# A decoder trunk on one core: attention's last combination moved forward within u's projection, and v's gelu taken over four token tiles at once

## The chip, the cores and the metric

One core of a Trainium2 chip runs the whole program. The metric is the device time of one execution in microseconds, here the median of several runs; a profiled execution of the same program gives the trace from which all rows come. Engine names are those of the profile: PE is TensorE (matmuls), PEld its weight loads, ACT is ScalarE, DVE is VectorE, POOL is GpSimd, SP is the engine that issues the DMAs.

## The reference: what is computed

The program is a trunk of two residual layers on 1024 tokens of width 1024, in float32. The change lies in the mixer of the first layer. It projects the normalised input to five parts of 512 columns, u, v, q, k and vb. From u and v it makes a gated product, from q, k and vb a mixture of attention branches, and one output projection takes both, side by side:

```python
def chunked_gmlp(u, v, ln_g, ln_b, w_s, b_s):
    ...
    vn = layer_norm(v, ln_g, ln_b).reshape(Bn, nc, A_CHUNK, A_GROUPS, A_GROUP_DIM)
    ...
    mixed = jnp.einsum('gts,bnsgc->bntgc', ws, vn) + b_s.astype(jnp.float32).T[:, :, None]
    return u.astype(jnp.float32) * mixed.reshape(Bn, S, A_WIDTH)

def even_mixer(h, w_in, a_ln_g, a_ln_b, a_ws, a_bs, q_g, k_g, w_out):
    ...
    a_out = chunked_gmlp(jax.nn.gelu(u, approximate=False), jax.nn.gelu(v, approximate=False),
                         a_ln_g, a_ln_b, a_ws, a_bs)
    ...
    for window, dilation in B_BRANCHES:
        o_r, l_r = dilated_branch(qh, kh, vh, window, dilation)
    ...
    wts = jax.nn.softmax(jnp.stack(lses), axis=0)
    ...
    return jnp.concatenate([a_out, b_out], axis=-1).astype(h.dtype) @ w_out
```

Heads are worked off in four pairs of two. Two kinds of score blocks remain after merging branches: near ones (128 neighbouring tokens and those before) and dilated ones (every fourth token). The combination weighs the near output and the dilated output of a pair by the exponentials of their log-denominators.

## The kernel before

Tokens lie in eight tiles of 128 (n = 0 to 7). Each matmul operand in float32 is split into a high and a low part in a format that TensorE multiplies in one pass, and three of the four products are summed (PASSES, line 40). So one token tile times one 1024x512 weight is 24 matmuls of 128x512 (mm_tok, lines 182 to 191), and every weight or activation that TensorE reads costs ScalarE a cast (the high part, line 100 or 105) and VectorE a subtraction (the low part, line 101 or 106).

The last stage of the first mixer, which the change touches, runs from 272 to about 410 us:

- gmlp (574 to 610) projects v, tile by tile, into PSUM (pv). consume evacuates each tile with a gelu on ScalarE (line 591), and VectorE makes the layer norm of it: statistics (593, 595), a power on POOL (141), then three passes (597, 598, 600) into mx, of which there are two, one per half (four token tiles). When a half is full, eight small matmuls with the causal weights (pm, line 605) mix the tokens of each chunk, one per channel group, and VectorE adds the bias back into mx (606). pm shares two PSUM banks with attention's scores.
- The dilated score blocks of the last head pair run at the same time (dilated, 737; unit, 650): scores on TensorE (sc3d, 641), mask and row maximum on VectorE (646), exponentials on ScalarE (sm3d, 647), transposes on TensorE (pP3d, 661), a copy (pT3d, 664 or 666), the products with the values (po3d, 669), and after four blocks a copy to ot3d (748). ot3d goes to DRAM and comes back in token order as on (750, 788).
- u_proj (612 to 621) projects u into pu, evacuates with a gelu (ut, 616) and multiplies it into mx (617). At a chosen tile it calls last, which combines the last head pair: minima and differences (cM, cE, 759 and 762), an exponential on ScalarE (763), weights (770 to 773), the two scalings on POOL and VectorE (776), the sum (778), and a DMA to bcat (779).
- out_first (432 to 454) is the first half of the output projection. For each tile a DMA reads attention's half from bcat (cat, 1122), TensorE transposes mx and cat (pc, 442), the result is split into hq, and 24 matmuls (po, 190) follow. bcat has two halves of four token tiles each, and a cat tile holds columns of all four head pairs, so it needs the last pair's combination.

ScalarE has gelu and exponential in different function tables, and an ACT_TABLE_LOAD stands in its row wherever one follows the other. Copies and casts stand there without one.

The order of the work is not that of the code: a scheduler interleaves the independent chains on each engine, and the code's order only ranks them. An instruction marked keep_in_program_order is held back to its place in the code; the first step of the combination (cM) is marked so. Each engine then works off its own list strictly in order. The DMA issues of SP are one such list too.

Of the kernel before, what the change touches and what calls it, by code (L numbers as in the profile page):

```python
# [9 lines left out]
F32 = mybir.dt.float32  # L10
# [3 lines left out]
AF = mybir.ActivationFunctionType  # L14
ALU = mybir.AluOpType
# [4 lines left out]
P = 128  # L20
# [6 lines left out]
GROUPS = 8  # L27
# [19 lines left out]
def flat(t):  # L47
    return t.rearrange("p a b -> p (a b)")
# [7 lines left out]
def trunk(ctx: ExitStack, tc: tile.TileContext, a, out):  # L56
    nc = tc.nc
    V, A, G, T, Q = nc.vector, nc.scalar, nc.gpsimd, nc.tensor, nc.sync
# [5 lines left out]
    small = ctx.enter_context(tc.tile_pool(name="small", bufs=4, reuse_waits="tile"))  # L64
# [72 lines left out]
    def inv_rms(ssq, cols, n, name, r=None):  # L137
        if r is None:
            r = small.tile([P, cols], F32, tag="rs%d" % cols, name=name)
        G.tensor_scalar(r, ssq, 1.0 / n, EPS, op0=ALU.mult, op1=ALU.add)  # L140
        G.tensor_tensor(r, r, mhalf[:, :cols], op=ALU.pow)
        return r
# [431 lines left out]
    def gmlp(ps, gm):  # L574

        wv = load_half(a["w_vu"][0], "wv", g0)
        lnG = gm.tile([P, 512], F32, name="lnG")
        Q.dma_start(lnG, a["ln_g"].partition_broadcast(P))
        lnB = gm.tile([P, 512], F32, name="lnB")
        Q.dma_start(lnB, a["ln_b"].partition_broadcast(P))  # L580
        bs = gm.tile([P, GROUPS], F32, name="bs")
        Q.dma_start(bs, a["a_bs"])
        ws = gm.tile([P, GROUPS, P], F32, name="ws")
        Q.dma_start(ws, a["a_ws"])

        G.affine_select(out=ws, in_=ws, compare_op=ALU.is_ge, fill=0.0, base=0,
                        pattern=[[0, GROUPS], [1, P]], channel_multiplier=-1)

        def consume(n, pj):
            gv = gm.tile([P, 512], F32, tag="gv", bufs=2, name=f"gv{n}")  # L590
            A.activation(gv, pj, AF.Gelu, scale=r0[:, n : n + 1])
            st = small.tile([P, 6], F32, tag="bn", name=f"bn{n}")
            V.bn_stats(st, gv)
            mv = small.tile([P, 2], F32, tag="mv", name=f"mv{n}")
            V.bn_aggr(mv, st)
            r = inv_rms(mv[:, 1:2], 1, 1, f"lr{n}")
            V.tensor_scalar(gv, gv, mv[:, 0:1], r, op0=ALU.subtract, op1=ALU.mult)
            V.tensor_mul(gv, gv, lnG)
            half, j = n // 4, n % 4
            V.tensor_add(mx[half][:, j, :], gv, lnB)  # L600
            if j == 3:
                for g in range(GROUPS):
                    gc = mx[half][:, :, g * 64 : g * 64 + 64]
                    pm = ps.tile([P, 4, 64], F32, tag="sc", name=f"pm{half}{g}")
                    T.matmul(pm, ws[:, g, :], gc, start=True, stop=True)
                    V.tensor_scalar(gc, pm, bs[:, g : g + 1], None, op0=ALU.add)

        mx = [gm.tile([P, 4, 512], F32, name=f"mx{h}") for h in range(2)]
        proj512(ps, wv, "pv", consume)
        return [mx[n // 4][:, n % 4, :] for n in range(NT)]  # L610

    def u_proj(ps, gm, mixed, last):

        def consume(n, pj):
            t = gm.tile([P, 512], F32, tag="gv", bufs=2, name=f"ut{n}")
            A.activation(t, pj, AF.Gelu, scale=r0[:, n : n + 1])
            V.tensor_mul(mixed[n], mixed[n], t)
            if n == 4:
                last()

        proj512(ps, load_half(a["w_vu"][1], "wu", g0), "pu", consume)
# [489 lines left out]
    ps = banks(pss, mm=3, pt=2)  # L1111
# [148 lines left out]
```

## Time and profile before

| | us |
|---|---|
| median of 3 runs | 2196.88 |
| the runs | 2193.66 to 2197.9 |
| the profiled execution, its own time | 2195.83 |
| its span, first to last instruction | 2194.0 |
| TensorE busy | 2147.0 |
| VectorE busy | 1533.2 |
| ScalarE busy | 1042.7 |
| GpSimd busy | 489.0 |

The mean granted TensorE clock is 0.994. The rows below are read so: in the list of waits, who waited for whom, the total, how often, the longest; in the list in time, start, length, engine, line, operation, output and inputs, shapes, count, and in brackets the idle time before it with what ended it; in the groups, busy time, mean in ns, and the idle time ahead of them. f32 transposes and small products count two rows per instruction.

### The profile page before, as it was taken

The numbers are of one execution on the slowest core, as the hardware profiler recorded it, in microseconds if no ns is written. First come the engines' busy times: TensorE is split into PE (matmuls) and PEld (weight loads), VectorE is DVE, ScalarE is ACT, GpSimd is POOL, SyncE is SP. The second block draws the span as 40 slices with busy tenths as digits, with TensorE's granted clock in tenths as the row PEclk, the third lists the DMA queues.
The fourth block names the chain that finished last, engine by engine and source line by source line (L and its number), as shares of the span: only waits on it lengthen the run. The fifth ranks groups of instructions, "written<-read, shape, count | busy, mean of one in ns | idle before, by whom it ended". The sixth has DMA issues, their size and how long they took to land.

```text
span 2194.0 us, 29873 instructions
## 1 busy us (share of the span) xinstructions
PE 2147.0 (98%) x10508; PEld 1816.2 (83%) x10508; DVE 1533.2 (70%) x2459; ACT 1042.7 (48%) x2006; POOL 489.0 (22%) x519
## 2 busy tenths in 40 slices
PE   8999999899999999999999999999999999999999
PEld 8999987687888888878889788878788888888887
DVE  5566653567888788855577777667787878885554
ACT  6555664245444444444454455534544444454443
POOL 4444410003334342200010011110232424320000
PEclk9999999899999999999999999999999999999999
DMA  4122212565544444585563123377544454457555
GB/s 148 47 72 81 78 35 59 179 247 189 163 158 158 154 154 159 187 291 179 204 236 113 68 97 104 104 258 265 194 145 153 158 165 157 168 176 268 204 195 203
DMA packets 157254, 349.59 MB, mean 159 GB/s; under 512 B 17408, under 2 KB 54272, under 8 KB 156720
## 3 DMA queue, kind: packets, MB, share of 16 engines
q1 hardware_dynamic: 157104, 347.68, 46.9%
q8 instruction: 83, 1.36, 0.3%
q14 instruction: 67, 0.55, 0.1%
HBM read 239.02 MB, written 108.59 MB: 158 GB/s over the span
## 4 chain that ended last, share of the span: by engine, by line
PE 88%; DVE 4%; DMA 3%; ACT 3%; issue 1%; POOL 1%; SPq 0%; ACTq 0%; DVEq 0%
PE puB L290 11%; PE pgB L290 11%; PE po L190 7%; PE pj L190 6%; PE pgC L290 5%; PE puC L290 5%; PE pv L190 5%; PE pdB L397 5%; PE pdC L397 5%; PE pdO L397 4%; PE puA L290 3%; PE pgA L290 2%; PE pdP L397 2%; PE pdQ L397 2%; PE pBq L972 2%; PE pu L190 2%
## 5 line engine op out<-in xcount | busy, mean ns | idle before, releaser
L101 DVE TENSOR_TENSOR da<-ar,da 128x512 fp32r<-128x512 f32 x154 | 106.3, 690 | 156.2 <-ACT da L100 156.0
L100 ACT CAST da<-ar 128x512 fp32r<-128x512 f32 x154 | 95.9, 623 | 209.4 <-PE pdC L397 90.7
L190 PE MATMUL po<-wo,hq 128*128 128x512 f32 x768 | 186.4, 397 | 0.6 <-DVE hq L101 0.3
L190 PEld LDWEIGHTS po<-wo,hq 128*128 128x128 f32 x768 | 142.5, 189 | 30.2 <-DVE hq L101 1.4
L190 PE MATMUL pj<-wq,hq 128*128 128x384 f32 x768 | 157.8, 352 | 2.3 <-ACT vN L701 1.3
L190 PE MATMUL pv<-wv,hq 128*128 128x512 f32 (+2 forms) x768 | 141.1, 340 | 2.4 <-DVE b L1004 1.6
L190 PEld LDWEIGHTS pj<-wq,hq 128*128 128x128 f32 x768 | 135.3, 195 | 4.0 <-ACT vN L701 2.1
L397 PE MATMUL pdB<-dw,da 128*128 128x512 f32 x528 | 136.2, 391 | 0.9 <-ACT dw L100 0.9
L397 PE MATMUL pdC<-dw,da 128*128 128x512 f32 x528 | 135.8, 390 | 0.0
L190 PEld LDWEIGHTS pv<-wv,hq 128*128 128x128 f32 x768 | 118.7, 189 | 17.6 <-DVE b L1004 2.1
L397 PEld LDWEIGHTS pdB<-dw,da 128*128 128x128 f32 x528 | 98.7, 188 | 22.2 <-ACT dw L100 1.3
L397 PEld LDWEIGHTS pdC<-dw,da 128*128 128x128 f32 x528 | 99.0, 188 | 20.5
L256 POOL TENSOR_TENSOR S1g<-rg 128x512 f32<-128x512 f32 x20 | 29.3, 1464 | 384.2 <-DMA wsd<-D 325.0
L101 DVE TENSOR_TENSOR dw<-wr,dw 128x512 fp32r<-128x512 f32 x154 | 105.8, 687 | 10.7 <-ACT dw L100 10.4
L140 POOL TENSOR_SCALAR rn<-ssq 128x1 f32<-128x1 f32 x24 | 9.5, 397 | 461.3 <-ACT h L148 245.3
L397 PE MATMUL pdO<-dw,da 128*128 128x512 f32 x396 | 102.2, 389 | 0.2 <-DVE dw L101 0.2
L100 ACT CAST dw<-wr 128x512 fp32r<-128x512 f32 x154 | 95.0, 617 | 15.3 <-DMA wr<-in_w_dn 7.0
L397 PEld LDWEIGHTS pdO<-dw,da 128*128 128x128 f32 x396 | 74.3, 188 | 16.0 <-DVE dw L101 0.6
L319 DVE SCALAR_TENSOR_TENSOR t<-g,cw,t 128x1022 f32<-128x1022 f32 x44 | 75.6, 1719 | 0.1
L318 DVE SCALAR_TENSOR_TENSOR t<-g,cw,t 128x1023 f32<-128x1023 f32 x44 | 58.3, 1325 | 16.4 <-ACT t L317 16.4
L303 DVE TENSOR_TENSOR g<-g,s1g 128x512 f32<-128x512 f32 x22 | 16.2, 737 | 73.9 <-ACT s1g L302 73.9
L320 ACT ACTIVATE t<-t 128x1024 f32<-128x1024 f32 x44 | 46.7, 1061 | 29.8 <-DVE t L319 29.6
(1070 smaller groups left out, 5405.9 us busy)
## 6 DMA issues: line engine op xcount, KB each, us to landing
ar<-actd SPq DMA_DIRECT2D x70, 512.0 KB, 3.5
rd<-in_w_down SPq DMA_DIRECT2D x44, 512.0 KB, 3.6
wsd<-D SPq DMA_DIRECT2D x88, 256.0 KB, 2.6
rg<-in_w_gate SPq DMA_DIRECT2D x42, 512.0 KB, 3.6
ru<-in_w_up SPq DMA_DIRECT2D x42, 512.0 KB, 4.6
wr<-wsd SPq DMA_DIRECT2D x40, 512.0 KB, 4.5
actd<-t SPq DMA_DIRECT2D x66, 256.0 KB, 2.1
wr<-in_w_dn SPq DMA_DIRECT2D x30, 512.0 KB, 5.0
```

The lines of the kernel that those rows point to most:

```text
L100: (hi or A.copy)(dst[0], src)
L101: (lo or V.tensor_sub)(dst[1], src, f32(dst[0]))
L140: G.tensor_scalar(r, ssq, 1.0 / n, EPS, op0=ALU.mult, op1=ALU.add)
L190: T.matmul(o, L[i], R[jj][:, sl], start=(k == 0 and (ii, jj) == PASSES[0]), stop=(k == nk - 1 and (ii, jj) == PASSES[-1]))
L256: G.tensor_tensor(sums[name], x, y, op=op)
L290: T.matmul(o, L[ii][:, j * P : j * P + P], right[p][:, jj, j, :], skip_group_check=more, start=(not more and j == 0 and (ii, jj) == PASSES ...
L303: V.tensor_add(C22, C22, s1)
L318: V.scalar_tensor_tensor(t[:, 1:], g[:, : S - 1], w(1), t[:, 1:], op0=ALU.mult, op1=ALU.add)
L319: V.scalar_tensor_tensor(t[:, 2:], g[:, : S - 2], w(0), t[:, 2:], op0=ALU.mult, op1=ALU.add)
L320: A.activation(t, t, AF.Silu)
L397: T.matmul(o, L[ii][:, t * P : t * P + P], R[jj], skip_group_check=more, start=start and not more and (ii, jj) == PASSES[0], stop=stop and ...
L972: T.matmul(o, L[ii][:, j * P : j * P + P], right[p][:, jj, j, :], skip_group_check=more, start=(not more and j == 0 and (ii, jj) == PASSES ...
```

## The change

Three things change. The raw projection of v is copied (with its scale) into mx, and one gelu of 128x2048 follows when a half is full; the layer norm of its four tiles comes after it. The second half's gelu is marked to be held back to its place in the code, which is behind the attention of the last pair. u's gelus get a tag of their own with five buffers (they shared two with v's), and last is called behind tile 1 in place of tile 4.

```diff
         def consume(n, pj):
-            gv = gm.tile([P, 512], F32, tag="gv", bufs=2, name=f"gv{n}")
-            A.activation(gv, pj, AF.Gelu, scale=r0[:, n : n + 1])
-            st = small.tile([P, 6], F32, tag="bn", name=f"bn{n}")
-            V.bn_stats(st, gv)
-            mv = small.tile([P, 2], F32, tag="mv", name=f"mv{n}")
-            V.bn_aggr(mv, st)
-            r = inv_rms(mv[:, 1:2], 1, 1, f"lr{n}")
-            V.tensor_scalar(gv, gv, mv[:, 0:1], r, op0=ALU.subtract, op1=ALU.mult)
-            V.tensor_mul(gv, gv, lnG)
             half, j = n // 4, n % 4
-            V.tensor_add(mx[half][:, j, :], gv, lnB)
-            if j == 3:
-                for g in range(GROUPS):
...
+            A.activation(mx[half][:, j, :], pj, AF.Copy, scale=r0[:, n : n + 1])
+            if j < 3:
+                return
+            ge = A.activation(flat(mx[half]), flat(mx[half]), AF.Gelu)
+            if half:
+                tc.keep_in_program_order(ge)
+            for j in range(4):
+                gv = mx[half][:, j, :]
+                st = small.tile([P, 6], F32, tag="bn", name=f"bn{half}{j}")
+                V.bn_stats(st, gv)
+                mv = small.tile([P, 2], F32, tag="mv", name=f"mv{half}{j}")
+                V.bn_aggr(mv, st)
+                r = inv_rms(mv[:, 1:2], 1, 1, f"lr{half}{j}")
+                V.tensor_scalar(gv, gv, mv[:, 0:1], r, op0=ALU.subtract, op1=ALU.mult)
+                V.tensor_mul(gv, gv, lnG)
+                V.tensor_add(gv, gv, lnB)
+            for g in range(GROUPS):
...
-            t = gm.tile([P, 512], F32, tag="gv", bufs=2, name=f"ut{n}")
+            t = gm.tile([P, 512], F32, tag="ut", bufs=5, name=f"ut{n}")
             A.activation(t, pj, AF.Gelu, scale=r0[:, n : n + 1])
             V.tensor_mul(mixed[n], mixed[n], t)
-            if n == 4:
+            if n == 1:
                 last()
```

What the scheduler makes of it is seen in the engines' lists. First ScalarE around v's last tile and u's first. Before (gv7 is the gelu of v's last tile, sm3d1xx the exponentials of the second dilated half):

```order
L591 ACT_TABLE_LOAD
L591 ACTIVATE gv7_4314<-pv7_4289,r0_84 128x512
L105 ACTIVATE wu3_1_4379<-wu3r_4374,g0_83 128x512
L647 ACT_TABLE_LOAD
L647 ACTIVATE sm3d101_3883,ot3d1_3870<-sm3d101_3883,ot3d1_3870 128x128
L647 ACTIVATE sm3d110_3895,ot3d1_3870<-sm3d110_3895,ot3d1_3870 128x256
L748 COPY ot3d0_3781<-po3d0_3782 128x4x128
L647 ACTIVATE sm3d111_3903,ot3d1_3870<-sm3d111_3903,ot3d1_3870 128x256
```

The changed kernel at the same place (lines are five higher there):

```order
L591 ACTIVATE mx1_4005<-pv7_4253,r0_84 128x512
L105 ACTIVATE wu3_1_4373<-wu3r_4368,g0_83 128x512
L594 ACT_TABLE_LOAD
L594 ACTIVATE mx1_4005<-mx1_4005 128x2048
L652 ACT_TABLE_LOAD
L652 ACTIVATE sm3d100_3876,ot3d1_3870<-sm3d100_3876,ot3d1_3870 128x128
L669 COPY pT3d03_3861<-pP3d03_3844 128x512
L652 ACTIVATE sm3d101_3883,ot3d1_3870<-sm3d101_3883,ot3d1_3870 128x128
L652 ACTIVATE sm3d110_3895,ot3d1_3870<-sm3d110_3895,ot3d1_3870 128x256
L621 ACT_TABLE_LOAD
L621 ACTIVATE ut0_4401<-pu0_4376,r0_84 128x512
L753 COPY ot3d0_3781<-po3d0_3782 128x4x128
```

One gelu of four tiles stands where the eighth small one stood; all eight exponentials of the second dilated half come behind it, and u's first gelus stand between them, with a table load at each turn. From v's first tile to u's last, ScalarE's list holds 21 table loads before and 11 now.

Second, VectorE where the last combination begins. Before (pm1x are the mixed groups of the second half, ut4 the gelu of u's fifth tile):

```order
L606 TENSOR_SCALAR mx1_4005<-pm16_4344,bs_3999 128x4x64
L606 TENSOR_SCALAR mx1_4005<-pm17_4347,bs_3999 128x4x64
L617 TENSOR_TENSOR mx1_4005<-mx1_4005,ut4_4519 128x512
L759 TENSOR_TENSOR cM30_4522<-ot3n0_3177,on30_3959 128x8
L617 TENSOR_TENSOR mx1_4005<-mx1_4005,ut5_4579 128x512
```

In the changed kernel:

```order
L611 TENSOR_SCALAR mx0_4004<-pm07_4172,bs_3999 128x4x64
L622 TENSOR_TENSOR mx0_4004<-mx0_4004,ut0_4401 128x512
L622 TENSOR_TENSOR mx0_4004<-mx0_4004,ut1_4429 128x512
L764 TENSOR_TENSOR cM30_4432<-ot3n0_3177,on30_3959 128x8
L622 TENSOR_TENSOR mx0_4004<-mx0_4004,ut2_4489 128x512
L622 TENSOR_TENSOR mx0_4004<-mx0_4004,ut3_4517 128x512
```

The combination's first step moved ahead of u's third multiplication, and ahead of every bias pass of the second half.

Third, VectorE at the hand-over to the output projection (wo are its weights, hq00 and hq10 the split transposes of its first tile). Before:

```order
L101 TENSOR_TENSOR wo02_1_4695<-wo02r_4690,wo02_1_4695 128x512
L101 TENSOR_TENSOR wo03_0_4700<-wo03r_4698,wo03_0_4700 128x512
L617 TENSOR_TENSOR mx1_4005<-mx1_4005,ut7_4635 128x512
L101 TENSOR_TENSOR wo03_1_4703<-wo03r_4698,wo03_1_4703 128x512
L101 TENSOR_TENSOR hq00_85<-pc00_4660,hq00_85 128x4x128
```

In the changed kernel:

```order
L101 TENSOR_TENSOR wo03_0_4694<-wo03r_4692,wo03_0_4694 128x512
L611 TENSOR_SCALAR mx1_4005<-pm17_4341,bs_3999 128x4x64
L622 TENSOR_TENSOR mx1_4005<-mx1_4005,ut4_4545 128x512
L622 TENSOR_TENSOR mx1_4005<-mx1_4005,ut5_4573 128x512
L622 TENSOR_TENSOR mx1_4005<-mx1_4005,ut6_4601 128x512
L622 TENSOR_TENSOR mx1_4005<-mx1_4005,ut7_4629 128x512
L101 TENSOR_TENSOR wo03_1_4697<-wo03r_4692,wo03_1_4697 128x512
L101 TENSOR_TENSOR hq00_85<-pc00_4654,hq00_85 128x4x128
```

The last bias pass and all four multiplications of the second half now stand between the weights' splits and the first split of hq; on TensorE the last pm stands behind u's last matmul, directly ahead of the first pc.

More of the change, by code (lines that the diff above doesn't have):

```diff
@@ L589, in consume @@
         def consume(n, pj):
-            gv = gm.tile([P, 512], F32, tag="gv", bufs=2, name=f"gv{n}")
-            A.activation(gv, pj, AF.Gelu, scale=r0[:, n : n + 1])
-            st = small.tile([P, 6], F32, tag="bn", name=f"bn{n}")
-            V.bn_stats(st, gv)
-            mv = small.tile([P, 2], F32, tag="mv", name=f"mv{n}")
-            V.bn_aggr(mv, st)
-            r = inv_rms(mv[:, 1:2], 1, 1, f"lr{n}")
-            V.tensor_scalar(gv, gv, mv[:, 0:1], r, op0=ALU.subtract, op1=ALU.mult)
-            V.tensor_mul(gv, gv, lnG)
-            half, j = n // 4, n % 4
-            V.tensor_add(mx[half][:, j, :], gv, lnB)
-            if j == 3:
-                for g in range(GROUPS):
[L603 to L606, printed above, removed]
+            half, j = n // 4, n % 4
+            A.activation(mx[half][:, j, :], pj, AF.Copy, scale=r0[:, n : n + 1])
[15 more added lines that the diff above has]
+            for g in range(GROUPS):
+                gc = mx[half][:, :, g * 64 : g * 64 + 64]
+                pm = ps.tile([P, 4, 64], F32, tag="sc", name=f"pm{half}{g}")
+                T.matmul(pm, ws[:, g, :], gc, start=True, stop=True)
+                V.tensor_scalar(gc, pm, bs[:, g : g + 1], None, op0=ALU.add)
         mx = [gm.tile([P, 4, 512], F32, name=f"mx{h}") for h in range(2)]
```

## The prediction

> **What bounds the kernel now.** The page's head comes first.
>
> ```profile
> span 2194.0 us, 29873 instructions
> PE 2147.0 (98%) x10508; PEld 1816.2 (83%) x10508; DVE 1533.2 (70%) x2459; ACT 1042.7 (48%) x2006; POOL 489.0 (22%) x519
> ```
>
> TensorE is the bound, so an edit on other engines gains only what TensorE idles, or runs slowly, because of them. The change touches the stretch from v's projection (272 us) to the first output tiles (about 410 us). The second view is the waits on TensorE there: who waited for whom, total, times, longest.
>
> ```profile
> PE pc L442 <- DMA cat<-bcat: 9.3, 1, 9.3
> PE pP3d L661 <- ACT sm3d L647: 3.3, 3, 2.0
> PE pu L190 <- ACT ut L616: 0.9, 1, 0.9
> PE pv L190 <- ACT gv L591: 0.5, 2, 0.3
> PE pv L190 <- ACT vN L701: 0.3, 1, 0.3
> ```
>
> So 14.3 us are lost there, 9.3 of them in one wait: the transposes of the first output tile need attention's half (cat), which a DMA reads from bcat. Third, TensorE in order of time (start, length, work; idle before it and its releaser in brackets).
>
> ```profile
> 310.32 0.39 PE L661 MATMUL pP3d<-ident,sm3d 128*128 128x128 f32 x2
> ...
> 338.66 0.47 PE L661 MATMUL pP3d<-ident,sm3d 128*128 128x128 f32 x1 [2.04 <-ACT sm3d L647]
> ...
> 339.64 4.56 PE L190 MATMUL pu<-wu,hq 128*128 128x512 f32 x15
> ...
> 368.94 4.59 PE L190 MATMUL pu<-wu,hq 128*128 128x512 f32 x19 [0.88 <-ACT ut L616]
> ...
> 393.56 0.60 PE L442 MATMUL pc<-ident,mx 128*128 128x128 f32 x4
> 403.41 1.12 PE L442 MATMUL pc<-ident,cat 128*128 128x128 f32 x4 [9.25 <-DMA cat<-bcat]
> ...
> 408.63 5.14 PE L190 MATMUL po<-wo,hq 128*128 128x512 f32 x19
> ```
>
> The reader is to see that equal rows last unequally: 19 matmuls take 4.59 us at 368.94 (0.24 us each) and 5.14 at 408.63; 15 take 4.56 at 339.64, where 0.24 each makes 3.62. The fourth view, by stretches, says why: its PEclk column is the granted clock (third from the end, ahead of DMA share and GB/s).
>
> ```profile
> 336.00:338.00 2.00, 0.62 (x4) 0.38 (x3) 1.77 (x5) 1.98 (x3) 0.19 (x1) 1.00 0.86 277
> 338.00:341.00 3.00, 2.34 (x7) 2.00 (x8) 2.34 (x6) 2.97 (x11) 0.55 (x1) 0.52 0.78 266
> ...
> 396.30:403.40 7.10, 0.00 (x0) 0.00 (x0) 2.93 (x5) 0.00 (x0) 0.00 (x0) 0.50 0.96 292
> 403.40:409.60 6.20, 5.94 (x19) 4.65 (x20) 1.98 (x3) 2.24 (x4) 0.00 (x0) 0.50 0.96 375
> 409.60:413.60 4.00, 4.00 (x18) 3.22 (x17) 0.69 (x1) 0.00 (x1) 0.00 (x0) 0.98 0.26 67
> ```
>
> After the 2.04 us gap the clock is half (0.52) for 3 us; after the long gap it stays half for 6.2 us of work. A gap thus costs its length and some slow matmuls behind it.
>
> **The combination, moved.** It is the chain that ends in the 9.25 us. Its stations now, and the DMA groups (KB each, us to landing):
>
> ```profile
> 359.26 0.59 ACT L748 COPY ot3d<-po3d 128x512 f32<-128x512 f32 x1 [5.23 <-PE po3d L669]
> ```
> ```profile
> 362.39 1.52 SPq L788 DMA_DIRECT2D on<-od  x2
> 393.23 0.36 SPq L779 DMA_DIRECT2D bcat<-ot3n  x1
> ...
> 397.82 0.47 SPq L1122 DMA_DIRECT2D cat<-bcat  x1
> ```
> ```profile
> 386.53 0.16 DVE L759 TENSOR_TENSOR cM<-ot3n,on 128x8 f32<-128x8 f32 x1
> ```
> ```profile
> cat<-bcat SPq DMA_DIRECT2D x4, 256.0 KB, 5.6
> ...
> on<-od SPq DMA_DIRECT2D x2, 264.0 KB, 3.3
> ```
>
> The data (on) is back at 362.39 + 1.52 + 3.3 = 367.2, but VectorE's first step (cM) starts at 386.53, behind u's fifth multiplication. From there to cat's landing at 403.4 it is 16.9 us. The order of the changed kernel puts cM behind u's second multiplication. That stands 75 u-matmuls and 8 small matmuls (pm) before the end of u: 75 x 0.24 + 8 x 0.25 = 20 us, less one bias pass and two multiplications (about 1.8 us), so 18 us ahead of it. If u ends at 387.4 (below), cM starts at 369.4. What it waits for: the last dilated outputs come 102 u-matmuls and 11 pm before that end, 27.2 us, so at 360.2; their copy ends near 361.0, and the round trip that takes 7.3 us now (359.85 to 367.2) ends at 368.3. That is 1 us of margin. Even if the rest again takes 16.9 us, cat lands at 386.3, before its transposes at 388.0. The 9.25 us go. Queued behind cM on VectorE are u's third and fourth multiplications and the bias passes that free pm's banks; a late "on" would hold these. On SP the loads of the second output half (wo10r to wo13r) now come behind cat; they are needed only near 452 us, and TensorE is busy without a break until then, so I cost that at nothing.
>
> **v's gelu in blocks of four.** Its rows on ScalarE, and four of the engine's list in time:
>
> ```profile
> L647 ACT ACT_TABLE_LOAD x9 | 11.5, 1283 | 12.1 <-DVE ot3d L646 6.5 <-DVE ot3n L646 5.5
> L591 ACT ACT_TABLE_LOAD x8 | 10.3, 1283 | 0.1
> ...
> L591 ACT ACTIVATE gv<-pv,r 128x512 f32<-128x512 f32 x8 | 5.5, 688 | 5.5 <-PE pv L190 5.5
> ...
> L616 ACT ACT_TABLE_LOAD x3 | 3.8, 1283 | 0.3 <-PE pu L190 0.3
> ```
> ```profile
> L320 ACT ACTIVATE t<-t 128x1024 f32<-128x1024 f32 x44 | 46.7, 1061 | 29.8 <-DVE t L319 29.6
> ```
> ```profile
> 299.93 1.28 ACT L647 ACT_TABLE_LOAD   x1 [5.49 <-DVE ot3n L646]
> 301.22 0.51 ACT L647 ACTIVATE sm3n<-sm3n,ot3n 128x256 f32<-128x256 f32 x1
> ...
> 302.33 1.28 ACT L591 ACT_TABLE_LOAD   x1
> 303.63 0.69 ACT L591 ACTIVATE gv<-pv,r 128x512 f32<-128x512 f32 x1
> ```
>
> With one more load ahead of cE there are 21 table loads; the order keeps 11, so ScalarE saves 12.8 us. That is not the gain, since TensorE never waits for ScalarE's sum, only for single exponentials. A raw copy out of PSUM in place of a gelu is no longer than 0.69 us. The 128x2048 gelu stands in no row: from 512 to 1024 columns a row grows from 0.688 to 1.061 us, so 1.81 us if that goes on, and at most 4 x 0.688 = 2.75; I take 1.81, as the rows of one form grow that way. The change does not wholly do what it says: the second gelu stands behind the first dilated half's last exponential, but eight exponentials (and the table loads between them and u's gelus) still follow it.
>
> Two places decide whether TensorE waits for an exponential.
>
> ```profile
> L593 DVE BATCH_NORM_STATS2 bn<-gv x8: 694/694/700, 279.4 to 336.2; 128x6 f32<-128x512 f32 x8
> ```
>
> First half: the last two exponentials of the near branch (301.22 to 302.33 now, behind a table load) move up by its 1.28 us and end at 301.0; copy (0.69), load, gelu end at 304.8, and pT's copy (0.59) at 305.4. The scores of the first dilated unit now wait on VectorE behind four statistics rows: 304.8 + 4 x 0.65 = 307.4, then its reductions and exponentials, which I put at the 1.1 us of that pair and 0.3 more: 308.8. TensorE wants them at 310.3, as now: 1.5 us of margin, 0.6 with the longer gelu. Second half: counted from the end of v's last matmul, copy, one weight split, load, gelu, load and exponential take 0.7 + 0.6 + 1.3 + 1.8 + 1.3 + 0.4 = 6.1 us. Ahead of the transpose that needs it the order gives TensorE 26 u-matmuls (6.2 us) and eight small groups (the pP3d row shows 0.39 for one, of which about 0.3 is its own time): 8.6 us. Margin 2.5. So the 3.3 us of pP3d, 0.9 of ut (its five buffers end the wait for a multiplication) and 0.3 of the second gv go: 4.5 us. With the 2.04 us gap goes its slow clock: 0.94 us at 339.64 and some 0.4 in the second before, 1.3.
>
> **The new wait at the hand-over.** The order puts the last pm behind u's last matmuls, so all four multiplications of the second half stand after it on VectorE, ahead of the split that frees the first transposes' bank. Rows:
>
> ```profile
> 366.40 0.92 DVE L606 TENSOR_SCALAR mx<-pm,bs 128x256 f32<-128x256 f32 x2 [3.18 <-PE pm L605]
> 367.42 1.29 DVE L617 TENSOR_TENSOR mx<-mx,ut 128x512 f32<-128x512 f32 x2
> ...
> 394.33 1.28 DVE L101 TENSOR_TENSOR wo<-wo01r,wo 128x512 fp32r<-128x512 f32 x2
> ...
> 404.75 1.29 DVE L101 TENSOR_TENSOR hq<-pc,hq 128x512 fp32r<-128x512 f32 x2 [5.53 <-ACT hq L100]
> ```
>
> From the last pm's start (u's end, U): its bias pass starts 0.6 us later behind the one before and a weight split, and ends at U + 1.4; four multiplications at 0.6 end at U + 3.8, one weight split at U + 4.45, the two hq splits at U + 5.1 and U + 5.7. ScalarE's last gelu, a weight cast and the first hq cast (0.7 + 0.6 + 0.6) let TensorE do two output matmuls by U + 2.4; then it waits to U + 5.1, 2.7 us. Transposes (0.55), three matmuls (0.7) and transposes again (0.55) later the steady run of 19 starts, at U + 6.9.
>
> **The sum.** U is 393.56 - 4.5 - 1.3 - 0.3 (the last pm now counts behind it) = 387.4. The run of 19 starts at 387.4 + 6.9 = 394.3. The new 2.7 us gap resembles the 2.04 us one, so I add its 1.3 to 1.4 us of slow clock: 395.7. Now it starts at 408.63 and loses 0.5 to the slow clock, which amounts to 409.1. Gain 13.4 us. Behind 410 us TensorE runs on without a wait, and what it loads comes as early as its buffers free, so the gain should last. The profiled execution took 2195.83 us (span 2194.0), 1 us below the median of 2196.88: 2195.83 - 13.4 = **2182.4**.
>
> [...]
>
> **Rivals.** (1) *The combination still ends late.* For: only 1 us of margin at cM, and 1.7 at cat. Against: 16.9 us includes a crowded DMA (0.96 share) that is idle there now. If the chain is 5 us longer, TensorE waits 3.3 us and pays 1.3 for the clock: 2187. Chance 0.10. (2) *The block gelu holds up exponentials.* For: margins of 0.6 to 2.5 us, four statistics rows in the way. Against: the order leaves matmuls between. Two waits of 2 us with 1.4 of clock each: 2189. Chance 0.08. (3) *Slower: ScalarE's alternation becomes the bound.* Six table loads stand between the exponentials of the second dilated half and u's first three gelus, two more at the first half. If each change costs d beyond 1.28 us, TensorE is held 8d less margins of 4.0, and four gaps cost 5.2 of clock. 8d - 4.0 + 5.2 eats 13.4 at d = 1.5, and beyond it the kernel is slower (2200 at d = 2). For: nine loads waited 12.1 us for VectorE's reductions, 1.3 each. Against: a gelu follows its load's end (303.61) after 0.02 us, and the loads' waits cost only where TensorE has nothing else. Chance 0.10, 0.06 of it slower by over 0.2% and the rest within.
>
> [...]
>
> **How the numbers follow.** My forecast, 2182.4, has 0.72, with 2178.5 to 2186 as its own range (no slow clock and run-to-run spread below; some longer gap above). With rivals 1 and 2 the range is **2178.5 to 2190**. About 0.2% (4.4 us) is what a measurement can tell from no change: faster 0.87 (forecast, rival 1, most of rival 2), same 0.07, slower 0.06.
>
> **What would show it.** Right: no wait of pc for cat; no wait of pP3d; cM near 369 us; 11 table loads; one gap of 2 to 3 us at the first output tile, released by VectorE's hq split; the clock at full from 336 to 388. Wrong: cM waiting on the DMA of "on" with pm held behind it; pP3d waiting near 310 or 335 us; a clock that stays at half beyond 400 us; or a wait behind 410 us that takes the gain back.

## The result and the profile after

| | before | after |
|---|---|---|
| median of 5 runs each (us) | 2197.45 (2193.66 to 2201.47) | **2184.7** (2180.82 to 2188.17) |
| ratio of after to before, 95% interval | | 0.9945 (0.9925 to 0.9965) |
| the same kernel measured again (e11) | | 0.9945 (0.9932 to 0.9959) |
| profiled execution, its span (us) | 2195.83, 2194.0 | 2181.74, 2180.0 |

The kernel became faster by about 12 us; the forecast was 2182.4, within 2178.5 to 2190. The time came out near the forecast partly by luck: the gain up to the output stage is 4 us larger than I worked out, and about as much is lost again behind it, in a place that I had costed at nothing.

The page's head of the changed kernel, then its waits on TensorE between 271 and 412 us and those between 412 and 560 us (line numbers from L606 on are 5 higher than before):

```profile
span 2180.0 us, 29848 instructions
...
PE 2140.4 (98%) x10508; PEld 1812.2 (83%) x10508; DVE 1530.1 (70%) x2459; ACT 1034.8 (47%) x1998; POOL 490.1 (22%) x519
```
```profile
PE pc L442 <- DVE hq L101: 1.7, 1, 1.7
PE pc L442 <- DVE mx L611: 0.7, 1, 0.7
PE po L190 <- ACT hq L100: 0.2, 1, 0.2
```
```profile
PE pt L162 <- DVE xt L152: 3.7, 2, 3.3
PE pgB L290 <- DVE hq L101: 1.3, 1, 1.3
```

No wait of pc for cat is left, none of pP3d for an exponential, none of pu for ut. What came instead is small at the hand-over (1.7 and 0.7), and new behind it: pt, the transposes of the output stage's normalised rows, waits 3.7 us for xt; before it waited 0.6 in the same stretch.

**The combination.** SyncE's and VectorE's rows of the changed kernel, in time:

```profile
357.74 1.17 SPq L793 DMA_DIRECT2D on<-od  x2
...
371.69 0.96 SPq L784 DMA_DIRECT2D bcat<-ot3n  x2
375.32 0.33 SPq L1127 DMA_DIRECT2D cat<-bcat  x1
```
```profile
364.51 0.16 DVE L764 TENSOR_TENSOR cM<-ot3n,on 128x8 f32<-128x8 f32 x1
```

cM starts at 364.51 in place of 386.53, with no idle time before it, so "on" was there already; cat's load is issued 9 us before its transposes (384.36 below).

**The hand-over.** TensorE in order of time, from u's last matmuls on:

```profile
382.82 0.59 PE L610 MATMUL pm<-mx,ws 128*128 128x256 f32 x2
384.08 0.44 PE L442 MATMUL pc<-ident,mx 128*128 128x128 f32 x2 [0.67 <-DVE mx L611]
384.36 0.38 PE L442 MATMUL pc<-ident,cat 128*128 128x128 f32 x2
...
385.41 0.73 PE L190 MATMUL po<-wo,hq 128*128 128x512 f32 x2 [0.24 <-ACT hq L100]
387.82 0.44 PE L442 MATMUL pc<-ident,mx 128*128 128x128 f32 x2 [1.67 <-DVE hq L101]
...
389.37 4.61 PE L190 MATMUL po<-wo,hq 128*128 128x512 f32 x19
```

The new gap is there, and its releaser is the predicted one: VectorE makes four multiplications of 2.5 us in all ahead of the hq split. But the run of 19 takes 4.61 us and not before's 5.14, and the granted clock is 1.00 from 387.8 to 392.0 us: no slow clock followed.

**Where the lead is lost again.** SyncE, VectorE and TensorE of the changed kernel near 450 us, and SyncE's waits there:

```profile
449.67 0.33 SPq L497 DMA_DIRECT2D xt<-xd  x1
```
```profile
SPq L497 <- DMA xd<-xh: 5.8, 1, 5.8
```
```profile
454.12 0.69 DVE L429 TENSOR_TENSOR xt<-xt,po 128x512 f32<-128x512 f32 x1 [10.67 <-DMA xt<-in_x]
```
```profile
460.41 1.56 PE L162 MATMUL pt<-ident,xt 128*128 128x128 f32 x12 [3.29 <-DVE xt L152]
```

The same three places of the kernel before:

```profile
461.94 0.44 SPq L497 DMA_DIRECT2D xt<-xd  x1
```
```profile
SPq L497 <- DMA xd<-xh: 0.3, 1, 0.3
```
```profile
475.89 1.47 PE L162 MATMUL pt<-ident,xt 128*128 128x128 f32 x12
```

SyncE holds the load of xt for 5.8 us behind a transfer that reads xh, where it waited 0.3 before. TensorE, 17 us ahead by then, runs into the late xt.

**Positions against the start of v.** Executions differ by up to 4 us at the start of v's projection (267.65 to 271.90 us in the traces below), in a part of the program that no kernel here changes, so spans mislead by that much. The table therefore counts from v's first matmul: how much earlier than in the kernel before TensorE reaches the 60th output matmul (17 to 19 us behind the first), the 12th matmul of pgC (in the first feed-forward block) and the program's last matmul. All are worked out from the timelines. The last column carries the chances of 1600 us more.

| kernel | time against before (95%) | at the 60th po | at pgC | at the end |
|---|---|---|---|---|
| after | 0.9945 (0.9925 to 0.9965) | +17.6 | +13.0 | +11.8 |
| e11 after, again | 0.9945 (0.9932 to 0.9959) | +17.6 | +11.3 | +10.1 |
| e1 move alone | 0.9939 (0.9925 to 0.9953) | +10.7 | +10.8 | +9.6 |
| e2 gelu alone | 1.0016 (1.0006 to 1.0027) | +3.7 | -4.4 | -4.2 |
| e3 pad alone | 1.0007 (0.9997 to 1.0017) | +0.2 | -1.0 | +1.6 |
| e4 lnG, lnB in ut's buffers | 0.9929 (0.9916 to 0.9942) | +17.6 | +14.2 | +12.3 |
| e5 e4, multiplications on GpSimd | 0.9931 (0.9919 to 0.9944) | +18.8 | +16.1 | +11.7 |
| e6 e4, half the stores | 0.9930 (0.9916 to 0.9943) | +17.6 | +16.2 | +14.8 |
| e7 e4, late raw loads | 0.9951 (0.9938 to 0.9963) | +17.6 | +9.2 | +8.3 |
| e8 e5 and e7 | 0.9950 (0.9937 to 0.9962) | +18.8 | +12.1 | +10.1 |
| e9 after, two ut buffers | 0.9934 (0.9920 to 0.9948) | +17.7 | +17.1 | +15.8 |
| e10 e4, slow gelu | 0.9935 (0.9923 to 0.9948) | +17.7 | +12.1 | +12.5 |
| e12 e9 with the pad | 0.9940 (0.9925 to 0.9956) | +17.7 | +13.0 | +12.7 |

The column at the 60th output matmul repeats to 0.1 us between executions of different kernels with the same edits, which the total time does not.

### The profile page after: what moved, and what is told of

The parts are those of the page before. It is cut to its first block, busy times and chain, and to the rows that moved or that the text cites. A ratio compares the mean times of both kernels' runs of the same rounds, so it can differ in the third digit from the quotient of the medians.

```text
span 2180.0 us, 29848 instructions
## 1 busy us (share of the span) xinstructions
PE 2140.4 (98%) x10508; PEld 1812.2 (83%) x10508; DVE 1530.1 (70%) x2459; ACT 1034.8 (47%) x1998; POOL 490.1 (22%) x519
## 4 chain that ended last, share of the span: by engine, by line
PE 72%; DMA 3%; DVE 2%; ACT 1%; issue 1%; POOL 0%; SPq 0%; DVEq 0%; ACTq 0%
PE puB L290 11%; PE pgB L290 11%; PE pgC L290 5%; PE puC L290 5%; PE pdB L397 5%; PE pdC L397 5%; PE pv L190 4%; PE pdO L397 4%; PE po L190 3%; PE puA L290 3%; PE pgA L290 2%; PE pdQ L397 2%; PE pdP L397 2%; PE pBq L977 2%; PE pBr L977 2%; DMA xd<-xt 1%
```

## The experiments

My theory after the two traces: the gain is cat's wait and the waits on exponentials, as forecast; the give-back comes from addresses. With ut's five buffers in place of gv's two the pool gm is three tiles of 2 KB a partition wider, the pool behind it (op0) moves, and xt's first buffer now shares addresses with an xh tile that a transfer still reads. The rivals: the move alone makes the whole gain; the two halves add up; and the give-back comes from transfers that crowd when TensorE is early.

**e1, the move alone.**

```diff
-            if n == 4:
+            if n == 1:
                 last()
```

> This kernel makes only the first half of the change: the last combination behind u's second tile; v's gelus stay eight small ones. My theory: the gain has two parts that add up at the hand-over, 9.25 us for the wait on cat, and 4.5 us of waits on exponentials and gelus with 1.3 us of clock, and some 4 us of it are lost again near 460 us, by a load of xt that waits for a transfer of xh's, because the five ut buffers shift the addresses of a later pool. Then here: no wait of pc for cat; the waits of pP3d near 335 us stay (3 to 4 us); no wait of pt for xt above 1 us near 460 us; the run of 19 output matmuls starts about 9 us earlier than before's 408.6, at 399 to 400; time 9 us below before, about 0.996 of it. Since after gives 4 us back and this does not, it should come within 3 us of after. Rival A: the block gelu brings nothing by itself and the move is the whole gain; then this kernel is as fast as after without its loss, 13 to 16 us below before. Rival B: the loss near 460 us comes from TensorE being early and the transfers crowded, not from addresses; then it shows here too, in proportion to the 9 us, and the time is 5 to 6 us below before.

Measured 2182.24 us (2179.99 to 2184.39), 0.9939 of before. Its waits on TensorE between 271 and 412 us:

```profile
PE pP3d L661 <- ACT sm3d L647: 3.3, 3, 2.0
PE po L190 <- ACT hq L100: 0.9, 1, 0.9
PE pu L190 <- ACT ut L616: 0.9, 1, 0.9
```

The wait for cat is gone, those on exponentials stay, and the lead of 10.7 us at the 60th output matmul is kept to the feed-forward block (10.8), as the first theory has it. The lead is the 9.25 us and, net of small new waits, about 1.4 us, which I put down to the half clock behind that wait in before (0.50 from 403.4 to 409.6 us). The median is 11.4 us below before's on that chip (13.4 by the ratio), more than the 9 that I gave; in the traced execution 4.2 us of the lead stood already at v's start. As a kernel it is as fast as the whole change, whose second half adds 7 us and then loses 4.6.

**e2, the gelu alone**: the changed kernel with `if n == 4` again.

> This kernel makes only the second half of the change: raw copies, block gelus and five ut buffers, with the last combination again behind u's fifth tile. My theory: TensorE's waits before 340 us go as in after, but u ends earlier while the combination still starts behind the last bias pass, so the wait of pc for cat grows from 9.25 to about 15 or 16 us and eats the gain: the run of 19 starts at 406 to 410 us against 408.6. Then the xt load still gives 3 to 4 us back near 460 us, so the time is 0 to 4 us above before (1.000 to 1.002 of it). Rival A (the two halves simply add up): wait for cat about 9 us as before, time 5 to 6 us below before, less the 4 us near 460 us if that comes from addresses.

Measured 2197.57 us (2193.87 to 2203.81), 1.0016 of before: slower. The waits on TensorE, and the first pt:

```profile
PE pc L442 <- DMA cat<-bcat: 14.0, 1, 14.0
```
```profile
476.69 2.82 PE L162 MATMUL pt<-ident,xt 128*128 128x128 f32 x12 [4.61 <-DVE xt L152]
```

The halves do not add up: u ends 7 us sooner, but the combination stands behind the last bias pass and cat's wait takes 4.7 of them. Alone the halves bring 10.7 and 3.7 us, together 17.6. The loss behind is 8.1 us here: 4.6 us more of waiting for xt than before, and half clock behind it (a granted clock of 0.50 from 476.7 to 481.7 us; 12 matmuls in 2.82 us, 1.47 in before).

**e3, the pad alone**: a tile that nobody uses, in before.

```diff
         wv = load_half(a["w_vu"][0], "wv", g0)
+        gm.tile([P, 3, 512], F32, name="gpad")
```

> The kernel before with nothing changed but a tile of 6 KB a partition in the pool gm that nobody reads or writes: what ut's five buffers do to the addresses, alone. My theory (addresses): all is as before up to 450 us, then the first load of xt waits 5 to 6 us for a transfer of xh (0.3 us before), TensorE's pt waits 2.5 to 3.5 us for xt near 475 us, and the time is 3 to 4 us above before (1.0015 of it). Rival B (the early TensorE and crowded transfers cause it): no such wait, time equal to before within 1 us.

Measured 2196.24 us (2192.75 to 2200.17), 1.0007 of before (0.9997 to 1.0017). SyncE's wait and pt's wait (0.6 in before):

```profile
SPq L497 <- DMA xd<-xh: 4.5, 1, 4.5
```
```profile
PE pt L162 <- DVE xt L152: 1.3, 2, 0.7
```

The wait of SyncE comes from dead memory alone, so it is the addresses. But TensorE waits only 0.7 us more, since it is 17 us later here than in after and most of the delay is covered. What the addresses cost depends on how early TensorE is; e12 measures that.

**e4, gm narrower again**: lnG and lnB are taken from ut's five buffers.

```diff
-        lnG = gm.tile([P, 512], F32, name="lnG")
+        lnG = gm.tile([P, 512], F32, tag="ut", bufs=5, name="lnG")
```

(lnB likewise.)

> The changed kernel, with the tiles of lnG and lnB taken from the same five buffers as ut, so that gm is two tiles narrower and the load of xt shares no address with xh's read. All instructions of the engines stay. My theory (addresses): the wait of pt for xt near 460 us (3.29 us in after) goes, and the time is about 4 us below after, so 16 us below before (0.9925 of it). Rival B (early TensorE, crowded transfers): the wait stays above 2 us and the time equals after's, 12 to 13 us below before. A risk beside both: u's first gelus may wait for lnG's buffer until the last norm has read it; that would show as a wait of pu for ut near 350 us.

Measured 2180.26 us (2176.39 to 2181.89), 0.9929 of before. SyncE's wait for xh's read is 0.3 us again, but TensorE still waits for xt, 2.5 us in all, and the lead falls from 17.6 to 14.2:

```profile
PE pt L162 <- DVE xt L152: 2.5, 2, 1.5
```
```profile
443.98 0.65 SPq L498 DMA_DIRECT2D xt<-in_x  x1
```
```profile
452.52 0.69 DVE L429 TENSOR_TENSOR xt<-xt,po 128x512 f32<-128x512 f32 x1 [9.77 <-DMA xt<-in_x]
```

The theory had the whole loss go; 1.2 us of it went. Every engine's list is the same as in the changed kernel, so in that order the shared addresses cost no more than this. xt is asked for in time and lands 8.5 us after its issue (443.98 to 452.52). In the changed kernel it was held for 5.8 us, but against v's start it was there only 0.8 us later (VectorE's step at 454.12 and 452.52, v at 269.68 and 268.92): most of the wait on SyncE was covered by the slow landing that xt has here without it. So there is something beside the addresses, and the next four runs looked for it in the transfers.

**e6, half the stores.** In the first feed-forward block's prepared sides:

```diff
-                Q.dma_start(sided[l][kind, p], f32(w))
+                if l:
+                    Q.dma_start(sided[l][kind, p], f32(w))
+                else:
+                    Q.dma_start(sided[l][kind, p][:, 0], f32(w[:, 0]))
...
```

> Base: e4. Left out: of the ten prepared sides of the first feed-forward block only the first half is stored to memory (256 KB each in place of 512), and it is read back twice, so the output is not the reference's; 2.56 MB less pass the DMA engines between 409 and 442 us, while every instruction of the compute engines stays. Theory C (the DMA engines' throughput): at 400 GB/s that is 6.4 us less of traffic; the first load of xt lands 5 to 6 us after its issue (8.5 in e4), the waits of pt for xt fall from 2.5 us to below 0.8, and the time is about 2 us below e4's. Rival (SP's order and VectorE's chain behind xt set it, not the traffic): the waits stay above 2 us and the time equals e4's within 0.7 us.

Measured 2180.4 us (2176.3 to 2180.56), 0.993 of before. VectorE's first step on xt, and TensorE's waits between 412 and 500 us:

```profile
447.95 0.69 DVE L436 TENSOR_TENSOR xt<-xt,po 128x512 f32<-128x512 f32 x1 [7.02 <-DMA xt<-xd]
```
```profile
PE pgB L297 <- DMA wg0p<-sided0g: 1.5, 1, 1.5
PE pt L162 <- issue: 1.0, 1, 1.0
```

pt no longer waits for xt, and the lead at pgC is 16.2 us against 14.2: with less traffic the loss is 1.4 us in place of 3.4. The time does not show it, 2180.4 against 2180.26: the difference is as small as the spread, and the traced execution of e6 began v 2.2 us later than e4's (271.12 and 268.92). So the traffic ahead of it makes xt late in e4.

**e5, the last four multiplications on GpSimd** (on top of e4).

```diff
-            V.tensor_mul(mixed[n], mixed[n], t)
+            (V if n < 4 else G).tensor_tensor(mixed[n], mixed[n], t, op=ALU.mult)
```

> Base: the kernel with lnG and lnB in ut's buffers (e4). There the addresses' wait is gone, but TensorE still waits 2.5 us for xt (1.46 and 1.0) where the kernel before waited 0.6. Changed here: u's last four multiplications are made on GpSimd, so VectorE comes 2.5 us sooner to the hq split at the hand-over. Theory C (the DMA engines are full, share 0.8 to 1.0, for the 20 us ahead of xt's landing, so xt comes by their throughput and a further lead of TensorE is lost in the wait for xt): the 1.67 us gap at the first transposes goes to below 0.3, the run of 19 output matmuls starts 1 to 1.7 us sooner against u's end, the waits of pt for xt near 456 us grow from 2.5 to 3.5 or more, and the time stays within 0.7 us of e4's. Rival (every microsecond of lead is kept, and e4's 2.5 us have a cause of their own): the waits of pt stay at 2.5 us and the time is 1 to 1.7 us below e4's.

Measured 2179.24 us (2177.79 to 2181.89), 0.9931 of before. The gap of 1.67 us falls to 0.5, the lead grows by 1.2 us, and pt waits 2.1 us for xt, not the 3.5 that I expected. So the strict form of the theory of traffic, that any further lead is lost, fell: the loads come earlier along with TensorE, and of 18.8 us of lead 16.1 reach the feed-forward block, a loss of 2.7 against e4's 3.4. In time e4 and e5 cannot be told apart.

**e7 and e8, the raw loads held back** (e7 on top of e4, e8 on e5), by a copy of one column of xt into each raw tile:

```diff
         raw = rawp.tile([P, D], F32, tag="raw", name=name)[:, :cols]
+        if name in ("rg0", "ru0", "rg2", "rg3") and len(gate) == 1:
+            G.tensor_copy(raw[:, :1], gate[0])
...
```

> Base: e4. The four raw loads of the first feed-forward weights (rg0, ru0, rg2, rg3, 512 KB each) are held back until the first xt has landed, by a one-column GpSimd copy from xt into each; SP's list then has xt's loads ahead of them. Theory C: 2 MB less stand ahead of xt, so xt's first pair lands about 3 to 5 us sooner after its issue than in e4 (8.5 us), the waits of pt for xt go (below 0.5 us), and the time is 2 to 2.5 us below e4's, unless the held loads come late for the first gate matmuls near 490 us, where a new wait of pgB for the weights would show. Rival (not the DMA): the waits stay and the time is that of e4 or above it.

> e5 and e7 together: u's last four multiplications on GpSimd and the raw loads held back. Theory C: with xt no longer late, the 1 to 1.7 us that e5 gains at the hand-over are kept, so the time is 1 to 1.7 us below e7's and 3 to 4 below e4's, about 0.991 of before. Rival (each microsecond of lead is kept anyhow): it stands to e7 as e5 to e4.

Measured 2183.27 us (2181.86 to 2186.2) and 2184.4 us (2179.94 to 2186.12), 0.9951 and 0.995 of before: 3 and 5 us above what they build on. In e7 VectorE and TensorE show why:

```profile
448.53 0.69 DVE L433 TENSOR_TENSOR xt<-xt,po 128x512 f32<-128x512 f32 x1 [4.31 <-DMA xt<-in_x]
462.41 0.75 DVE L156 TENSOR_SCALAR xt<-xt,rn 128x1024 f32<-128x1024 f32 x1 [5.66 <-DMA xd<-xt]
```
```profile
494.39 0.80 PE L294 MATMUL pgB<-hq,wg0p 128*128 128x512 f32 x1 [2.93 <-ACT hq L100]
```

xt lands 4.6 us after its issue in place of 8.5, as the theory said. But the copies that hold the loads waited until VectorE had normalised the first xt in its place (to 455.4 us), not only for its landing, and SyncE stood 6.0 us for them. The store of the second xt is behind them in SyncE's list, and VectorE's next step waits 5.66 us for it. Near 494 us VectorE has the weights' splits still to do ahead of the rows that the gate matmuls need, and TensorE waits 2.93 us. The traffic was moved, not removed.

**e9, two ut buffers** in the changed kernel.

```diff
-            t = gm.tile([P, 512], F32, tag="ut", bufs=5, name=f"ut{n}")
+            t = gm.tile([P, 512], F32, tag="ut", bufs=2, name=f"ut{n}")
```

> The changed kernel with two ut buffers in place of five; gm is then no wider than needed and the load of xt shares no address with xh's read. My step said that the five buffers end the 0.9 us wait of u for a multiplication (pu for ut). If that is so, this kernel shows waits of pu for ut or for mx of 1 to 3 us between 345 and 385 us, its run of 19 starts 1 to 3 us later than after's against the start of v, and what it wins near 460 us (1.3 us for the addresses, less crowding) gives that back: time within 2 us of e4's, 2179 to 2183. Rival: the buffers do nothing by themselves, only the block gelu counts; then no wait for ut shows and the time equals e4's or is below it.

Measured 2180.4 us (2177.5 to 2182.69), 0.9934 of before. Its waits on TensorE between 271 and 412 us, and between 412 and 500 us:

```profile
PE po L190 <- ACT hq L100: 0.9, 1, 0.9
PE pu L190 <- ACT ut L621: 0.6, 1, 0.6
...
PE pc L442 <- DVE hq L101: 0.2, 1, 0.2
```
```profile
PE pgB L290 <- DVE hq L101: 1.2, 1, 1.2
```

A wait of 0.6 us for ut is there, smaller than I gave, and it costs nothing on balance: with two buffers the order takes the second half's bias passes and multiplications earlier, so the gap of 1.67 us at the hand-over is gone. The lead at the 60th output matmul is the same, 17.7, and 17.1 of it reach the feed-forward block. Here nobody waits for xt, with the same traffic as e4.

**e12, e9 with the pad.** The tile of e3 is added to e9; the order of all engines stays that of e9, word for word.

> e9 (two ut buffers) plus the dead tile of 6 KB a partition in gm: the order of every engine is that of e9, and in SP's list the first load of xt alone gains a wait, for the transfer that reads xh. e9 has TensorE as far ahead as e4 at the start of the output stage (17.3 us against the start of v) and no wait of pt for xt at all. If the addresses cost what the lead lays open, SP waits 5 to 6 us for xd<-xh ahead of xt here (0.3 us in e9), xt lands about 2 to 3 us later, pt waits 2.5 to 4 us for xt, and the time is 3 to 5 us above e9's, 0.995 to 0.996 of before. If instead the losses near 460 us belong to crowded transfers and the wait on xh's read is mostly hidden behind them, pt waits below 1.5 us and the time is within 1.5 us of e9's, as the pad alone cost only 1.4 us in e3's trace.

Measured 2183.37 us (2176.65 to 2187.93), 0.994 of before. SyncE's wait (0.3 in e9) and TensorE's (none in e9):

```profile
SPq L497 <- DMA xd<-xh: 5.1, 1, 5.1
```
```profile
PE pt L162 <- DVE xt L152: 3.4, 2, 2.7
```

From the same lead of 17.7 us, e9 brings 17.1 to the feed-forward block and e12 13.0, the 13.0 of after. The one difference is dead memory. So at this lead and in e9's order the addresses cost 4.1 us (3.4 of waits for xt, less 0.7 of other waits, and by my estimate up to 1.7 of half clock behind the gap of 2.72: the granted clock is 0.50 from 460.75 to 462.75 us and 0.63 and 0.66 in the microseconds on either side). The times show less of it than I expected, 0.994 with an interval up to 0.9956, which overlaps e9's.

**e10, a slow gelu** on top of e4: two more passes over each half ahead of its gelu.

```diff
+            A.activation(flat(mx[half]), flat(mx[half]), AF.Copy)
+            A.activation(flat(mx[half]), flat(mx[half]), AF.Copy)
             ge = A.activation(flat(mx[half]), flat(mx[half]), AF.Gelu)
```

> Base: e4. Two more passes over each half (raw 128x2048 copies in place, about 1.9 us each) stand ahead of each block gelu, so ScalarE comes 3.8 us later to the exponentials behind it; nothing else changes. My theory of margins: in after, TensorE reached the first transposes behind the gelu about 2.0 us after their data in the first half and 1.3 us in the second, so 3.8 us turn into waits of pP3d of about 1.8 and 2.5 us, 4.3 in all, with up to 1.3 us of half clock behind each, and the run of 19 starts 4 to 6 us later against the start of v; the time is 3 to 7 us above e4's. Rival (ScalarE has far more room, and what counted was the place behind the last exponential): no wait of pP3d above 0.5 us and a time equal to e4's. Rival (each gap also throws back the chain through VectorE, as in my slower case): waits of 8 us and more, and the kernel near before's time.

Measured 2180.46 us (2179.29 to 2183.28), 0.9935 of before, as e4. No wait of pP3d appears, and the lead at the 60th output matmul is 17.7. ScalarE in the first half:

```profile
302.86 1.91 ACT L595 ACTIVATE mx<-mx 128x2048 f32<-128x2048 f32 x1
304.68 0.38 ACT L654 ACTIVATE sm3d<-sm3d,ot3d 128x128 f32<-128x128 f32 x1
...
306.04 1.28 ACT L596 ACT_TABLE_LOAD   x1
307.34 1.92 ACT L596 ACTIVATE mx<-mx 128x2048 f32<-128x2048 f32 x1
```

My margins of 1.3 and 2.0 us were no limit: the order put the first dilated exponentials ahead of the gelu, and 7.6 us more on ScalarE cost TensorE nothing up to the output stage. The run doesn't measure the margin in after's own order, but it shows that ScalarE has room in this stretch. Behind it pt waits 3.7 us for xt here and the lead falls to 12.1, with no address in the way (SyncE's wait for xh's read is 0.3).

**e11, the changed kernel again.**

> The changed kernel once more, on the chip of the other two, for a second trace. If the loss near 460 us is as told (the load of xt held 5.8 us by xh's read, and crowded transfers), the waits of pt for xt are 3 to 4 us again and the time is 1 to 4 us above e4's ratio, 0.9935 to 0.995 of before. If half clock behind the 1.9 us gap near 66 us is chance, it can come out either way here: full clock in the first trace of after, half in four of the nine others.

Measured 2182.98 us (2179.79 to 2187.13), 0.9945 of before; SyncE holds xt for 5.9 us, and pt waits:

```profile
PE pt L162 <- DVE xt L152: 4.4, 2, 3.7
```

The loss repeats (6.3 us of lead here, with a granted clock of 0.50 from 464.9 to 466.9 us behind the wait, and 4.6 in the first trace, with 1.00 from 460.4 to 465.4). On the clock my expectation miscounted: half clock followed the gap near 66 us in five of the nine other traces, not four; in this one it did too (0.53 from 68 to 70 us).

## Why the prediction was right, and where it was not

1. *The wait for cat goes* (9.25 us): right, and shown by e1 alone. The margin was larger than my 1 us: the second load of on landed at 361.6, 2.9 us ahead of cM, and cat was loaded well ahead of its transposes. The first rival fell.
2. *The waits on exponentials and gelus go* (4.5 us): right. From v's first matmul to the last pm, one row of before and one of after:

```profile
271.90:393.56 121.66, 116.80 (x585) 96.81 (x585) 60.61 (x153) 64.99 (x114) 16.05 (x29) 0.99 0.15 46
```
```profile
269.68:382.82 113.14, 112.97 (x583) 95.84 (x584) 61.82 (x155) 57.55 (x106) 17.43 (x29) 1.00 0.24 74
```

   TensorE's idle time falls from 4.9 to 0.2 us, against 4.5 forecast, and no wait of pP3d is left, so the second rival fell. Its busy time falls by 3.8 us, where I had 1.6 (1.3 of clock, 0.3 for the last pm that now counts behind). The other 2.2 us were mis-sized. Counted from each matmul's start to the next, the larger part of them lies in pm: 0.18 us for each before, where twenty of the 32 stand in rows of four and eight, and 0.13 after, where each pair stands between u's matmuls; why a row of them is slower was not tested. This term needs the first: e2 shows that without the move it brings 3.7 us and then costs more.
3. *The gelu of 128x2048 takes 1.81 us*: it takes 1.92, within the bounds; e10 makes ScalarE's part far longer and reaches the 60th output matmul as early, though in another order.
4. *The five ut buffers end the wait for ut*: true but worth nothing. e9 with two buffers reaches the same point at the same time, and the five buffers are what widens gm.
5. *The new wait at the hand-over, 2.7 us and slow clock behind it*: the wait is 0.67 and 1.67 us, the run of 19 starts 6.55 us behind the last pm (6.9 forecast), and the slow clock of 1.4 us did not come (1.00 from 387.8 to 392.0 us). That term was an estimate from a single gap, the one of 2.04 us; behind other short gaps half clock came or stayed away (last section).
6. *"Behind 410 us TensorE runs on without a wait, and what it loads comes as early as its buffers free, so the gain should last"*: this step failed. 4.6 us of 17.6 went, most of them by a late xt. Two delays lie over each other there. SyncE holds the load for the read of xh, because gm is wider: 1.2 us in the changed kernel's own order (e4, the same lists without the shared addresses), 4.1 where nothing else makes xt late (e12 against e9). The other is the traffic ahead of xt: e4 still loses 3.4 us, 1.4 with half the stores (e6). I had looked at the order of SyncE's list and not at the waits in it, which the address of a later pool sets, nor at how long a load takes to land behind the others. Of the loads wo10r to wo13r that I did cost at nothing, the trace after shows waits of 0.3 us in all (po for wo).
7. *The sum.* The run of 19 moved by 17.0 us against v's start, and with the 0.5 us of slow clock that it loses in before, 17.5 us stand against 13.4 forecast: 2.4 more from step 2, 0.35 and 1.4 from step 5. The two errors, 4.1 us too little and 4.6 us not foreseen, cancelled, which was luck.
8. *Slower, by ScalarE's alternation*: it did not come. ScalarE of the changed kernel:

```profile
298.92 1.28 ACT L594 ACT_TABLE_LOAD   x1
300.21 1.92 ACT L594 ACTIVATE mx<-mx 128x2048 f32<-128x2048 f32 x1
```

   The load ends at 300.20 and the gelu starts at 300.21, so nothing beyond the load is paid; and e10 adds 7.6 us to ScalarE without a wait of pP3d.

What stays open is why e4, with no address in the way, waits 2.5 us for xt and e9 does not, from the same lead and with the same transfers. e6 shows that less traffic ends it. Against v's start, e9 asks for xt's second half 0.9 us sooner than e4, and it takes 7.3 us to land in place of 8.4, so it is there 2.0 us sooner; in e10, as free of the shared addresses, it takes 9.1. What makes these landings differ no run here isolates.

e4, e5 and e9 have medians of 2179 to 2180 us, 0.993 of before, about 3 to 5 us below after's two medians; their intervals overlap with after's, so only the traces tell them apart. e9 is the simplest, a change of one number.

## What to carry to other kernels

An edit may be worth less than nothing alone (e2: 3.7 us, then a loss) and several microseconds beside another (e9 is 6 us ahead of e1 at the feed-forward block): look for what is late next before judging one by itself. When a buffer count grows, compare not only the order of the instructions but the waits of the transfers behind that pool: a tile that nobody uses cost 4 us in e12, where TensorE had become early, and nothing that the times show in e3, where it had not. Where executions differ by 4 us before the changed part begins, measure from the last unchanged point.

## What the runs showed of the hardware

In these traces the length of a gap alone does not settle whether half clock follows it. All fourteen traces of before, after and the experiments have the same gap of 1.88 to 1.91 us at 66 to 70 us, released by the same copy; here before and after in the windows behind it (the third number from the end is the granted clock):

```profile
68.00:72.00 4.00, 4.00 (x17) 4.00 (x16) 3.22 (x10) 1.19 (x5) 2.39 (x3) 0.57 0.65 180
```
```profile
68.00:72.00 4.00, 4.00 (x26) 3.96 (x25) 2.76 (x9) 1.19 (x5) 2.45 (x5) 1.00 0.75 208
```

Half clock followed in eight of the fourteen, for 3.4 us, beginning up to 2 us behind the gap; half of those 3.4 us, 1.7 us of time, is an estimate of what that alone costs at most. Of the other gaps of over 1.2 us in these traces (60 to 100 and 300 to 560 us), none of the fifteen up to 1.76 us was followed by it, one of 1.89 was, all six from 2.04 to 2.93 us were, the 3.29 of after was not (1.00 from 460.4 to 465.4 us), and the five from 3.71 to 13.96 were. The lengths overlap: one gap of 1.89 us was followed by half clock, the gap of 3.29 was not, and the same gap of 1.9 was in some executions and not in others.

The clock records of before and after show when it came. Up to 2150 us the granted clock is 0.50 in before from 68.45 to 71.87 us, 143.55 to 150.38, 338.11 to 341.52 and 396.13 to 409.79, in after from 141.25 to 148.08, and otherwise 1.00 from 20 us on. These stretches last one, two, one and four times 3.41 us, and two times; in before they start 22, 57 and 17 times 3.41 us apart. Laid out in such steps, the two traces have 1236 at full clock between 20 and 2150 us. In eleven of them TensorE was busy for 0.42 to 0.56 of the step; half clock came with the next step behind five (0.42, 0.50, 0.52 and 0.56 in before, 0.53 in after) and not behind six (0.53 in before, 0.50 to 0.54 in after). In the other 1225 it was busy for 0.68 or more, and half clock came behind none. The gap of 3.29 us in after lies across two steps, with TensorE busy for 0.54 and 0.50 of them; in e11, 2.3 of the 3.71 us lie in the 3.41 us ahead of its half clock, which starts near 464.0 us. That the place of a gap among these steps decides is my reading of two traces; it would let the same gap fall either way, as it did, and eleven steps do not prove it.
